# A list-scheduled hybrid encoder layer on one core: the steps that finish and store the output are given earlier due times, and in the last block of the down projection the B12 sums are made by accumulating DMAs

## The chip, the core and the metric

One core of one Trainium2 chip runs the whole layer. Its engines are TensorE (PE, with its weight loads, PEld), VectorE (DVE), ScalarE (ACT), GpSimd (POOL) and SyncE (SP); SP issues most DMAs, and POOL issues those that add into their destination. Each engine runs its instructions in the order in which they stand in the program, and waits for the others by semaphores. The metric is the device time of one execution in microseconds (us); the median of three runs counts.

## The reference, cut to what matters

```
mod = silu(c) @ w_ada + b_ada;  sh1, sc1, gt1, sh2, sc2, gt2 = split(mod, 6)
h = rmsnorm(x, g_norm_mix) * (1 + sc1) + sh1
proj = h @ w_in            # 2048 -> 1024 (RG-LRU) + 1024 (its gate) + 1024 (pooling)
y = concat(rg_lru(conv(xr)) * gelu(gr), pool_mixer(xp)) @ w_out
x = x + gt1 * y
h = rmsnorm(x, g_norm_ffn) * (1 + sc2) + sh2
f = (silu(h @ w_ffn_gate) * (h @ w_ffn_up)) @ w_ffn_down      # 2048 -> 5632 -> 2048
x = x + gt2 * f
return rmsnorm(x, g_norm_final)                                # (1, 512, 2048), float32
```

One sequence of 512 tokens, model width 2048, everything in float32. The change concerns the last line but one and the last: the product with w_ffn_down, the gate gt2, the residual sum and the final norm.

## The kernel before

**Products.** A float32 product is made of three passes on TensorE: each operand is split into `hi` (a rounded copy, made by ACT) and `lo` (the rest, made by DVE), and hi·hi, hi·lo and lo·hi are summed in PSUM (`mm3x`). The three FFN products go by `seven` (line 879): a block matrix product of 2 by 2 blocks in seven products instead of eight, called A11, n1, s2, n4, A12, n3 and A22 after their left operand. Each right operand is built in SBUF from four weight blocks B11, B12, B21 and B22 of 128 x 1024 elements (512 KB): `b11(i)` loads B11 into a buffer `araw` (`chain`) and splits its negative; `t1(i)` adds B12 to it and splits the sum; `t2(i)` adds B22, which lies in a buffer `raw` (`other`); `b22(i)` splits that; `t3(i)` adds B12 to it and splits; `b21(i)` loads B21 into `raw` and subtracts it in the chain; `t4(i)` splits what the chain has become. So B12 is added twice in each part i. `plus_b12` (line 916) has two ways for it: with `by_dma` a DMA issued by POOL adds the block from HBM into the buffer, without it SP loads the block into a `raw` buffer and DVE adds. The gate and up projections use the first way, the down projection the second. There are four `araw` buffers, six `raw`, and three each of `hi` and `lo`.

**The down projection** runs in four blocks of the 5632 inner channels (DOWN_BLOCKS 2, 3, 3, 3). The last block has three parts i, and it goes over the output in two halves `qp` of 1024 columns; a half is 7 products of 3 parts with 12 matmuls each, 252 matmuls of 128 x 512. The output lies in 16 tiles `fsum[t][q]` of 128 x 512 (t: 4 token tiles, q: 4 quarters of the columns; `qa`, `qb` are a half's two). In the names that follow the four tiles of q=1 are b_2454, b_2455, b_2446, b_2447, those of q=0 b_2436, b_2437, b_2478, b_2479, those of q=3 b_2506, b_2507, b_2498, b_2499, and those of q=2 b_2488, b_2489, b_2530, b_2531. `later_block` adds the products' PSUM banks to them, and in the last block, when a tile is complete, it calls `finish`: `residual` multiplies the tile by the gate (DVE) and adds x1 from HBM by an accumulating DMA of 256 KB (POOL); ACT sums the squares; DVE multiplies by the final norm's weight `gfin[q]`; and when the last quarter of a token tile is done, `norm` computes the factor 1/rms, scales the four tiles (one on DVE, three on ACT) and stores them (SP). For the last quarter, q=2, residual comes early and `finish` multiplies the product's PSUM bank by the gate and adds it. The gates (`gt_0` to `gt_3`) and `gfin` come by eight DMAs of 256 KB into buffers `blk`.

**The order.** The code does not run as written: `Program` records all instructions with an estimated cost, `deadlines` gives each a due time, counted back from what needs it, and `schedule` plays the engines forward in a model and always takes the instruction that can start first, among equals the one with the earlier due time. The result is one fixed order for each engine. A rule in `buffers` (line 269) bears on the DMAs into `blk`: `dma_free` is the time up to which the model has the DMA engines filled, `now` is the time of the queue that would issue, and while the first is over DMA_AHEAD = 4 us ahead of the second and the load isn't overdue, the load is not taken:

```
if op["dma"] and tag == "blk" and dma_free - now > self.DMA_AHEAD and late > 0.0 and not wide:
    return need, None
```

`wide` becomes true only when nothing else can go on any engine. The model charges a DMA from POOL at twice the time of one from SP.

Of the kernel before, what the change touches and what calls it, by code (L numbers as in the profile page):

```python
# [27 lines left out]
ADA_CHUNKS = (1, 1, 2, 2, 2, 2, 2, 2, 2)  # L28
GROUP_ENDS = (2, 8, 16)
HELD = 6  # L30
NFF = 5632 // 512
DOWN_BLOCKS = (2, 3, 3, 3)
BUFS = {"blk": 69, "raw": 6, "araw": 4, "hi": 3, "lo": 3, "acc": 6, "mm": 2}
# [3 lines left out]
class Program:  # L37
# [35 lines left out]

    def __init__(self, nc, bufs, spare):
        self.nc, self.bufs, self.spare = nc, bufs, spare
        self.ops, self.tags, self.in_order = [], {}, set()
        for q in self.QUEUES:
            setattr(self, q, self.Queue(self, q))

# [15 lines left out]
    def add(self, queue, method, args, kw):  # L95
        after, lead = kw.pop("after", None), kw.pop("lead", None)
        outs = list(args[:1]) + [kw[n] for n in ("out", "accum_out") if kw.get(n) is not None]
        ins = list(args[1:]) + [v for n, v in kw.items() if n not in ("out", "accum_out")] + [after]
        on_chip = lambda v: isinstance(v, bass.AP) and type(v.tensor).__name__ == "Tile"
        op = {"i": len(self.ops), "q": self.QUEUES[queue], "call": (queue, method, args, kw),  # L100
              "w": [self.region(v) for v in outs if on_chip(v)], "r": [self.region(v) for v in ins if on_chip(v)]}
        if op["q"] == "PE":
            op["w"] = [(name, 0, P, 0, 512) for name, *_ in op["w"]]
        op["tiles"] = list(dict.fromkeys(x[0] for x in op["w"] + op["r"] if x[0] in self.tags))
        op["t"], op["stream"] = self.cost(op["q"], method, args, kw, outs[0])
        reads = [v for v in ins if on_chip(v) and v.space not in (bass.MemoryType.PSUM, bass.MemoryType.DRAM) and v.shape[-1] > 1]
        op["dma"] = method == "dma_start"
        op["port"] = op["q"] == "POOL" and len(reads) > 0 and not op["dma"] or op["q"] == "DVE" and (
            len(reads) > 1 or len(reads) == 1 and method in ("tensor_scalar", "tensor_copy"))
        op["table"], op["lead"] = self.TABLES.get(kw.get("func")), lead  # L110
        self.ops.append(op)

    @staticmethod
# [41 lines left out]
    def deadlines(self):  # L155

        at = 0.0
        users, order, serves = {}, {}, {}
        for op in self.ops:
            op["due"] = 1e9  # L160
            if op["q"] == "PE":
                op["due"] = op["nominal"] = at
                at += op["t"]
            for name in op["tiles"]:
                tag = self.tags[name]
                if name not in users and tag != "blk":
                    tiles = order.setdefault(tag, [])
                    if len(tiles) >= self.bufs[tag]:
                        for i in users[tiles[-self.bufs[tag]]]:
                            serves.setdefault(i, []).append(op["i"])  # L170
                    tiles.append(name)
                users.setdefault(name, []).append(op["i"])
        before = [set(op["pred"]) for op in self.ops]
        for i, later in serves.items():
            for j in later:
                if j > i:
                    before[j].add(i)
        behind = [0] * len(self.ops)
        for js in before:
            for j in js:  # L180
                behind[j] += 1
        latest, queued, held = [at + 50.0] * len(self.ops), {}, {}
        heap = [(-latest[i], -i) for i, n in enumerate(behind) if not n]
        heapq.heapify(heap)
        while heap:
            _, i = heapq.heappop(heap)
            op = self.ops[i := -i]
            q, due = op["q"], latest[i]
            tag = self.tags.get(op["w"][0][0]) if q == "SP" and op["w"] else None
            if tag in ("raw", "araw"):  # L190
                due = queued[tag] = min(due, queued.get(tag, 1e9) - 0.6)
            op["due"] = min(op["due"], due - op["t"] - (self.SLACK if not op["dma"] else self.SLACK_DMA if q == "SP" else self.SLACK_SUM))
            if q in ("DVE", "ACT", "SP"):
                t = max(op["t"], self.DMA_ISSUE) if q == "SP" else op["t"] * self.LOAD
                op["due"] = held[q] = min(op["due"], held.get(q, 1e9) - t)
            for j in before[i]:
                latest[j] = min(latest[j], op["due"])
                behind[j] -= 1
                if not behind[j]:
                    heapq.heappush(heap, (-latest[j], -j))  # L200
        for op in self.ops:
            if op["lead"] is not None:
                op["due"] = op["lead"] - 1e3 + 1e-4 * op["i"]

# [158 lines left out]
def hybrid_trunk(ctx: ExitStack, tc: tile.TileContext, a: dict, out: bass.AP):  # L363
# [6 lines left out]
    nc = Program(tc.nc, BUFS, SPARE)  # L370
# [189 lines left out]
    proj = {}  # L560
    held = {n: mmps("acc") for n in range(HELD)}

# [145 lines left out]
    def pool_group(g):  # L708
# [16 lines left out]
        for j in range(2):  # L725
            ps = mmps()
            for k in range(2):
# [11 lines left out]
                  lead=3)  # L739
# [237 lines left out]
    left = []  # L977
# [71 lines left out]
    kept = None  # L1049
    for n in range(NFF):  # L1050
        f = gate_up(n, kept)
        kept = lambda n=n, f=f: keep(n, f)
# [5 lines left out]
    for bi, nb in enumerate(DOWN_BLOCKS):  # L1058
        last = bi == len(DOWN_BLOCKS) - 1
        left = []  # L1060
# [13 lines left out]
        for qp in range(2):  # L1074
# [67 lines left out]
            def later_block(step, banks, tiles=range(2)):  # L1142
                for j in tiles:
                    x, y = banks["X"][j], banks.get("Y", (None, None))[j]
                    if step == "P1":
                        add(j, qa, x, ALU.subtract)
                        if last and qp:
                            residual(j, qa)
                    elif step == "G5":
                        add(j + 2, qb, y)  # L1150
                    elif step == "G6":
                        add(j, qb, x)
                    elif step == "G3":
                        add(j, qb, y)
                    elif step == "G7":
                        add(j + 2, qb, x)
                    elif last and qp:
                        finish(*((j, qa, banks["Z"][j]) if step == "P2" else (j + 2, qa, x)))
                    elif step == "P2":
                        add(j, qa, banks["Z"][j])  # L1160
                    else:
                        add(j + 2, qa, x, ALU.subtract)
                    if last and (step in ("G3", "G7") or step in ("P2", "G4") and not qp):
                        finish(*{"G3": (j, qb), "G7": (j + 2, qb), "P2": (j, qa), "G4": (j + 2, qa)}[step])
# [5 lines left out]
            if last and qp:  # L1170
                for t in (2, 3):
                    residual(t, qa)
            seven(left, b, later_block if bi else first_block, False, by_tile=last and qp == 1, within=kept if not bi and not qp else None)
        n0 += nb

    nc.issue()
# [22 lines left out]
```

## Time and profile before

| | us |
|---|---|
| median of 3 runs | 1877.52 (1876.21 to 1879.55) |
| the profiled execution, its own time | 1870.78 |
| its span, first to last instruction | 1868.9 |
| PE busy | 1797.6 (96%) |
| DVE busy | 1540.0 (82%) |
| ACT busy | 935.9 (50%) |
| POOL busy | 196.3 (11%) |

The times below are counted from the start of the span of the profiled execution. A row of the timeline reads: start, duration, engine, line (every recorded instruction has the helper's line 359 before and 361 after), operation, output<-input, shape, count, and in brackets how long the engine had been idle and what ended that. A row of the waits reads: who waited for whom, total, times, longest. "DMA to landing" is the time from the issue of a DMA to its completion. PEclk is the granted clock of TensorE as a share of 2.4 GHz.

### The profile page before, as it was taken

The numbers are of one execution on the slowest core, as the hardware profiler recorded it, in microseconds if no ns is written. First come the engines' busy times: TensorE is split into PE (matmuls) and PEld (weight loads), VectorE is DVE, ScalarE is ACT, GpSimd is POOL, SyncE is SP. The second block draws the span as 40 slices with busy tenths as digits, with TensorE's granted clock in tenths as the row PEclk, the third lists the DMA queues.
The fourth block names the chain that finished last, engine by engine and source line by source line (L and its number), as shares of the span: only waits on it lengthen the run. The fifth ranks groups of instructions, "written<-read, shape, count | busy, mean of one in ns | idle before, by whom it ended". The sixth has DMA issues, their size and how long they took to land.

```text
span 1868.9 us, 22751 instructions
## 1 busy us (share of the span) xinstructions
PE 1797.6 (96%) x8011; PEld 1469.1 (79%) x8011; DVE 1540.0 (82%) x1974; ACT 935.9 (50%) x1221; POOL 196.3 (11%) x192
## 2 busy tenths in 40 slices
PE   3899998899999999999999999999999999999996
PEld 2687877688886888888788888888888888888875
DVE  5899998899969878678787867877678887878897
ACT  7435794422377555454454545545455543333345
POOL 0000054500001111111111111111110000000011
PEclk9999999999999999999999999999999999999998
DMA  9999755499945777788878778777799966947556
GB/s 304 315 359 321 227 175 184 142 334 342 359 146 104 192 201 213 209 207 214 221 191 226 208 205 214 210 202 199 171 273 318 339 218 195 328 155 263 194 143 180
DMA packets 285763, 429.97 MB, mean 230 GB/s; under 512 B 20760, under 2 KB 119760, under 8 KB 285648
## 3 DMA queue, kind: packets, MB, share of 16 engines
q1 hardware_dynamic: 259408, 378.17, 60.4%
q0 software_dynamic: 26240, 50.34, 16.2%
q8 instruction: 63, 1.03, 0.2%
q14 instruction: 52, 0.43, 0.1%
HBM read 378.63 MB, written 49.81 MB: 229 GB/s over the span
## 4 chain that ended last, share of the span: by engine, by line
PE 65%; DVE 15%; issue 9%; DMA 7%; ACT 2%; SPq 1%; POOL 1%; ACTq 0%; DVEq 0%; POOLq 0%
PE acc L359 62%; DVE b L359 10%; DVE lo L359 4%; DMA araw<-in_w_ada 3%; PE mm L359 3%; ACT b L359 2%; SPq L359 1%; DVE araw L359 1%; DMA b<-x 1%; DMA raw<-in_w_ffn_down 1%; ACT hi L359 1%; DMA b<-in_x 1%; DMA araw<-in_w_ffn_up 1%; DMA raw<-in_w_ffn_gate 0%; DMA araw<-in_w_ffn_gate 0%
## 5 line engine op out<-in xcount | busy, mean ns | idle before, releaser
L359 PE MATMUL acc<-hi,b 128*128 128x512 f32 x4208 | 1290.0, 392 | 1.6 <-DVE b L359 1.0
L359 PEld LDWEIGHTS acc<-hi,b 128*128 128x128 f32 x4208 | 789.7, 188 | 166.2 <-DVE b L359 2.5
L359 PE MATMUL acc<-lo,b 128*128 128x512 f32 x2104 | 803.1, 393 | 4.7 <-DVE lo L359 4.5
L359 ACT ACTIVATE hi<-raw 128x1024 fp32r<-128x1024 f32 (+2 forms) x297 | 306.5, 1034 | 436.6 <-PE acc L359 347.2
L359 PEld LDWEIGHTS acc<-lo,b 128*128 128x128 f32 x2104 | 395.3, 188 | 91.2 <-DVE lo L359 10.6
L359 DVE TENSOR_TENSOR lo<-raw,hi 128x1024 fp32r<-128x1024 f32 (+2 forms) x297 | 355.4, 1199 | 126.1 <-ACT hi L359 125.1
L359 ACT ACTIVATE hi<-araw 128x1024 fp32r<-128x1024 f32 x264 | 279.8, 1060 | 286.4 <-PE acc L359 268.9
L359 DVE TENSOR_TENSOR lo<-araw,hi 128x1024 fp32r<-128x1024 f32 x198 | 241.9, 1222 | 57.0 <-ACT hi L359 56.5
L359 DVE SCALAR_TENSOR_TENSOR b<-araw,c_act,b 128x512 f32<-128x512 f32 (+1 forms) x315 | 233.0, 746 | 8.0 <-DMA araw<-in_w_ada 4.7
L359 DVE TENSOR_TENSOR b<-b,b 128x512 f32<-128x512 f32 (+4 forms) x318 | 195.0, 634 | 14.2 <-ACT b L359 10.7
L359 PE MATMUL acc<-b,hi 128*128 128x512 f32 x608 | 189.2, 396 | 4.0 <-ACT hi L359 1.5
L359 ACT ACTIVATE b<-b 128x512 fp32r<-128x512 f32 (+2 forms) x223 | 128.6, 596 | 97.7 <-DVE b L359 54.9
L359 PEld LDWEIGHTS acc<-b,hi 128*128 128x128 f32 x608 | 114.3, 190 | 31.0 <-ACT b L359 3.5
L359 DVE SCALAR_TENSOR_TENSOR lo<-araw,hi 128x1024 fp32r<-128x1024 f32 x66 | 80.6, 1223 | 47.6 <-ACT hi L359 47.4
L359 PE MATMUL acc<-b,lo 128*128 128x512 f32 x304 | 116.1, 396 | 2.5 <-DVE lo L359 2.5
L359 POOL DMA_DIRECT2D araw<-in_w_ffn_up x44 | 53.1, 1209 | 557.8 <-DVE lo L359 390.4
L359 ACT ACTIVATE b<-acc 128x512 f32<-128x512 f32 x142 | 81.7, 593 | 53.9 <-PE acc L359 45.5
L359 DVE TENSOR_TENSOR araw<-araw,raw 128x1024 f32<-128x1024 f32 x88 | 106.9, 1220 | 0.6
L359 DVE SCALAR_TENSOR_TENSOR araw<-araw,raw 128x1024 f32<-128x1024 f32 x66 | 79.9, 1220 | 13.6 <-DMA raw<-in_w_ffn_gate 8.6
L359 POOL DMA_DIRECT2D raw<-in_w_ffn_up x44 | 53.0, 1204 | 334.4 <-DVE lo L359 332.9
L359 PE MATMUL mm<-b,hi 128*128 128x512 f32 x192 | 62.2, 404 | 10.4 <-ACT b L359 10.3
L359 PEld LDWEIGHTS acc<-b,lo 128*128 128x128 f32 x304 | 58.1, 191 | 15.8 <-DVE lo L359 3.8
(72 smaller groups left out, 872.8 us busy)
## 6 DMA issues: line engine op xcount, KB each, us to landing
araw<-in_w_ada SPq DMA_DIRECT2D x256, 256.0 KB, 4.6
raw<-in_w_ffn_down SPq DMA_DIRECT2D x88, 512.0 KB, 5.5
f<-b SPq DMA_DIRECT2D x154, 256.0 KB, 4.7
b<-f SPq DMA_DIRECT2D x154, 256.0 KB, 5.9
araw<-in_w_ffn_gate SPq DMA_DIRECT2D x44, 512.0 KB, 3.8
raw<-in_w_ffn_up SPq DMA_DIRECT2D x44, 512.0 KB, 4.2
araw<-in_w_ffn_up POOLq DMA_DIRECT2D x44, 512.0 KB, 7.0
raw<-in_w_ffn_gate SPq DMA_DIRECT2D x44, 512.0 KB, 5.7
```

Of the source, the lines that this page charges most:

```text
L359: getattr(getattr(self.nc, queue), method)(*args, **kw)
```

## The change

Three edits. (1) A constant END_EARLY = 60.0; while `nc.early` is set, recorded instructions carry it, and at the end of `deadlines` their due time is made 60 us earlier. It is set round the `finish` calls of the last half's steps P2 and G4, those that complete the four tiles of q=2 and call `norm`, so their products with the gate, squares, factors, scalings and output DMAs carry it. (2) The last block of the down projection is called with `by_dma` true: the 12 B12 blocks of its two halves are no longer loaded by SP and added by DVE, but added by 12 accumulating DMAs of 512 KB from POOL. (3) Nothing else is computed or left out.

```diff
+END_EARLY = 60.0
...
-        self.ops, self.tags, self.in_order = [], {}, set()
+        self.ops, self.tags, self.in_order, self.early = [], {}, set(), 0.0
...
-        op["table"], op["lead"] = self.TABLES.get(kw.get("func")), lead
+        op["table"], op["lead"], op["early"] = self.TABLES.get(kw.get("func")), lead, self.early
...
         for op in self.ops:
+            op["due"] -= op["early"]
             if op["lead"] is not None:
...
                     elif last and qp:
+                        nc.early = END_EARLY
                         finish(*((j, qa, banks["Z"][j]) if step == "P2" else (j + 2, qa, x)))
+                        nc.early = 0.0
...
-            seven(left, b, later_block if bi else first_block, False, by_tile=last and qp == 1, within=kept if not bi and not qp else None)
+            seven(left, b, later_block if bi else first_block, last, by_tile=last and qp == 1, within=kept if not bi and not qp else None)
```

What this does to the orders shows at three places. First DVE, in the last block's first half, as its last B21 blocks and the A22 operands are split; the tiles b_24xx are those of q=1 and q=0, b_2954 is gate gt_1 and b_2911 the norm weight of q=1. Before:

```order
L359 TENSOR_TENSOR b_2455<-b_2455,acc_2929 128x512
L359 TENSOR_TENSOR b_2454<-b_2454,b_2954 128x512
L359 TENSOR_TENSOR lo_2972<-raw_2970,hi_2971 128x1024
L359 TENSOR_TENSOR b_2455<-b_2455,b_2954 128x512
L359 TENSOR_TENSOR lo_2975<-raw_2973,hi_2974 128x1024
L359 TENSOR_TENSOR b_2446<-b_2446,acc_2917 128x512
L359 TENSOR_TENSOR b_2447<-b_2447,acc_2918 128x512
L359 TENSOR_TENSOR b_2446<-b_2446,b_2954 128x512
L359 TENSOR_TENSOR lo_2978<-raw_2976,hi_2977 128x1024
L359 TENSOR_TENSOR b_2447<-b_2447,b_2954 128x512
L359 TENSOR_TENSOR b_2454<-b_2454,b_2911 128x512
```

The products with gate and norm weight stand between the splits here. Now the same tiles (the gate gt_1 is called b_2951) stand at the end of DVE's order, behind the very last split of the program, lo_3055 (the third part of the second half's A22 operand):

```order
L361 TENSOR_TENSOR lo_3053<-araw_2990,hi_3052 128x1024
L361 TENSOR_TENSOR b_2499<-b_2499,acc_2986 128x512
L361 TENSOR_TENSOR lo_3055<-araw_2993,hi_3054 128x1024
L361 TENSOR_TENSOR b_2454<-b_2454,b_2951 128x512
L361 TENSOR_TENSOR b_2455<-b_2455,b_2951 128x512
L361 TENSOR_TENSOR b_2446<-b_2446,b_2951 128x512
L361 TENSOR_TENSOR b_2447<-b_2447,b_2951 128x512
L361 TENSOR_TENSOR b_2454<-b_2454,b_2911 128x512
L361 TENSOR_TENSOR b_2455<-b_2455,b_2911 128x512
L361 TENSOR_TENSOR b_2446<-b_2446,b_2911 128x512
L361 TENSOR_TENSOR b_2447<-b_2447,b_2911 128x512
L361 TENSOR_TENSOR b_2436<-b_2436,b_2973 128x512
```

All 12 tiles of q=1, 0 and 3 moved there in this pattern, four products with the gate and then four with the norm weight, and the four tiles of q=2 stand behind them. Second, SP's queue, where the gates and norm weights (gt, in_g_norm_final) are loaded. Before, the first of them stood among the loads of the last block's first half:

```order
L359 DMA b_2909<-f_1173 128x512
L359 DMA b_2954<-gt_1_1175 128x512
L359 DMA araw_2993<-in_w_ffn_down 128x2x512
L359 DMA raw_2957<-in_w_ffn_down 128x2x512
L359 DMA b_2913<-in_g_norm_final 128x512
L359 DMA b_2910<-in_g_norm_final 128x512
L359 DMA b_2911<-in_g_norm_final 128x512
L359 DMA b_2912<-in_g_norm_final 128x512
```

Now all eight follow the last weight block of the program (raw_3030, a B21 block of the second half):

```order
L361 DMA raw_3024<-in_w_ffn_down 128x2x512
L361 DMA raw_3027<-in_w_ffn_down 128x2x512
L361 DMA raw_3030<-in_w_ffn_down 128x2x512
L361 DMA b_2951<-gt_1_1175 128x512
L361 DMA b_2910<-in_g_norm_final 128x512
L361 DMA b_2911<-in_g_norm_final 128x512
L361 DMA b_2912<-in_g_norm_final 128x512
L361 DMA b_2913<-in_g_norm_final 128x512
L361 DMA b_2973<-gt_0_1174 128x512
L361 DMA b_3019<-gt_3_1177 128x512
L361 DMA b_2984<-gt_2_1176 128x512
L361 DMA out<-b_2498 128x512
```

The loads of gates and norm weights have moved behind all weight loads, next to the stores of the output. Third, POOL's queue behind the up projection. Before, the sixteen residual sums (x_t_q) followed at once; now the twelve B12 sums stand ahead of them, of which these are the last six:

```order
L361 DMA araw_2987<-in_w_ffn_down 128x2x512
L361 DMA araw_2990<-in_w_ffn_down 128x2x512
L361 DMA araw_2993<-in_w_ffn_down 128x2x512
L361 DMA raw_3004<-in_w_ffn_down 128x2x512
L361 DMA raw_3007<-in_w_ffn_down 128x2x512
L361 DMA raw_3010<-in_w_ffn_down 128x2x512
L361 DMA b_2454<-x_0_1_705 128x512
L361 DMA b_2455<-x_1_1_709 128x512
```

The first residual sum now comes behind the last B12 sum, which belongs to step G7 of the second half.

## Rows read from the trace of the kernel before

**Rows 1.** The profile's page: span; busy time and share of each engine

```profile
span 1868.9 us, 22751 instructions
...
PE 1797.6 (96%) x8011; PEld 1469.1 (79%) x8011; DVE 1540.0 (82%) x1974; ACT 935.9 (50%) x1221; POOL 196.3 (11%) x192
```

**Rows 2.** Stretches near the end: busy time by engine, PEclk, DMA share, GB/s

```profile
1820.00:1830.00 10.00, 10.00 (x45) 7.98 (x44) 9.86 (x12) 3.56 (x4) 1.35 (x2) 1.00 0.41 131
...
1840.00:1850.00 10.00, 9.03 (x32) 6.99 (x32) 10.00 (x16) 6.42 (x12) 2.39 (x3) 0.83 0.37 52
...
1860.00:1865.00 5.00, 0.00 (x0) 0.00 (x0) 2.05 (x8) 3.64 (x7) 0.00 (x0) 0.50 0.91 305
```

**Rows 3.** Timeline of PE in the last block

```profile
1755.04 0.62 PE L359 MATMUL acc<-hi,b 128*128 128x512 f32 x2
...
1755.72 0.62 PE L359 MATMUL acc<-hi,b 128*128 128x512 f32 x2
...
1797.30 0.50 PE L359 MATMUL acc<-lo,b 128*128 128x512 f32 x1 [0.84 <-DVE lo L359]
...
1840.63 0.73 PE L359 MATMUL acc<-lo,b 128*128 128x512 f32 x2 [2.01 <-DVE lo L359]
...
1842.17 1.48 PE L359 MATMUL acc<-hi,b 128*128 128x512 f32 x3
...
1856.66 0.39 PE L359 MATMUL acc<-hi,b 128*128 128x512 f32 x1
```

**Rows 4.** Timeline of ACT in the last block

```profile
1736.43 1.07 ACT L359 ACTIVATE hi<-araw 128x1024 fp32r<-128x1024 f32 x1 [1.21 <-PE acc L359]
...
1781.29 0.63 ACT L359 ACTIVATE b<-b 128x512 f32<-128x512 f32 x1 [3.00 <-DMA b<-x]
1781.82 0.19 ACT L359 ACTIVATION_READ_ACCUMULATOR b<-b 128x1 f32 x1
...
1860.99 2.72 ACT L359 ACTIVATE b<-b,s 128x512 f32<-128x512 f32 x4
```

**Rows 5.** Timeline of DVE in the last block

```profile
1732.08 1.23 DVE L359 SCALAR_TENSOR_TENSOR lo<-araw,hi 128x1024 fp32r<-128x1024 f32 x1 [1.49 <-ACT hi L359]
...
1777.94 0.68 DVE L359 TENSOR_TENSOR b<-b,b 128x512 f32<-128x512 f32 x1
...
1782.04 0.69 DVE L359 TENSOR_TENSOR b<-b,b 128x512 f32<-128x512 f32 x1 [1.68 <-ACT b L359]
...
1842.82 3.09 DVE L359 TENSOR_TENSOR b<-b,b 128x512 f32<-128x512 f32 x5
...
1851.38 1.21 DVE L359 TENSOR_TENSOR lo<-araw,hi 128x1024 fp32r<-128x1024 f32 x1
...
1858.32 0.69 DVE L359 TENSOR_TENSOR b<-b,b 128x512 f32<-128x512 f32 x1
```

**Rows 6.** Timeline of POOL: issues of residual sums

```profile
1778.92 0.86 POOL L359 DMA_DIRECT2D b<-x  x1 [2.07 <-DVE b L359]
...
1828.65 1.77 POOL L359 DMA_DIRECT2D b<-x  x2 [15.90 <-DVE b L359]
```

**Rows 7.** POOL DMAs to landing: residual sums, B12 into araw, into raw

```profile
DMA to landing us min/median/max: 4.0/4.9/7.7
...
DMA to landing us min/median/max: 5.8/7.0/11.4
...
DMA to landing us min/median/max: 5.9/6.2/11.8
```

**Rows 8.** The page: DMA queue, packets, MB, share of 16 engines

```profile
q0 software_dynamic: 26240, 50.34, 16.2%
```

**Rows 9.** Groups of DVE by line and form, 1737 to 1869 us

```profile
L359 DVE TENSOR_TENSOR araw<-araw,raw 128x1024 f32<-128x1024 f32 x11 | 13.2, 1220 | 0.0
...
L359 DVE TENSOR_TENSOR raw<-raw,raw 128x1024 f32<-128x1024 f32 x6 | 7.3, 1221 | 1.7 <-DMA raw<-in_w_ffn_down 1.7
```

**Rows 10.** Waits, 1700 to 1869 us

```profile
ACT b L359 <- DMA b<-x: 21.6, 9, 4.3
```

## The prediction, made before the changed kernel ran

> **What bounds the kernel now.** I read the page first: PE is busy for 96% of the span, DVE for 82%, POOL for 11% [rows 1]. So up to the end TensorE sets the time, and an edit that takes work from DVE can give back only what PE waits for DVE. I then went to the last block, the only place where the change moves much. The stretches show three phases [rows 2]: PE without a gap beside a DVE at 9.86 of 10 us, then 1840 to 1850 with PE at 9.03 and a granted clock of 0.83, then, from 1860 on, no PE at all, and the time goes to factors, scalings and stores. PE's timeline gives the size of the gaps: 0.84 us at 1797 and 2.01 us at 1841, both ended by a `lo` of DVE, and behind the second three matmuls take 1.48 us, where three normally follow each other in 0.68 (1755.04 to 1755.72) [rows 3]; the clock had been full until that gap and fell in the stretch that holds it, to a mean of 0.83, so part of it ran at 1.2 instead of 2.4 GHz. PE ends at 1856.66 + 0.39 = 1857.05. From there to the end of the span are 11.85 us.
>
> How much is there to win? ACT's split at 1736.43 waits for a buffer that PE gives up with its last matmul of the block before [rows 4], so the last block starts there. It has 2 halves x 7 products x 3 parts x 12 matmuls = 504, at 0.68/3 = 0.227 us [rows 3] 114.3 us: unhindered PE would end at 1850.7. The gaps of the whole last block are thus 6.4 us, and no more than that lies in a faster DVE.
>
> **The change: what it removes.** Twelve additions of 1.22 us leave DVE, 14.6 us [rows 9]; beside them PE is busy, so what they are worth is in the 6.4 us and is not counted twice. The second gap hangs on a raw block that comes late and is added on DVE; in the new order the block's B12 goes into its buffer by POOL, a product earlier. I take both gaps as gone.
>
> **What it adds on POOL.** Twelve accumulating DMAs of 512 KB. The 88 of this kind in the trace land 7.0 (into `araw`) or 6.2 us (into `raw`) after issue, 11.4 and 11.8 at most [rows 7]. Behind `t1` or `t3` waits the split, behind that PE. A product of three parts lasts 36 x 0.227 = 8.2 us, and the split of B11 ends at 1732.08 + 1.23 = 1733.3, 3.1 us before PE starts on it at 1736.4 [rows 4, 5]; so there are 11.3 us from the split to the next product. Needed are 0.3 us to the issue, 7.0 to landing, and 1.07 + 1.23 for the next two splits [rows 4, 5]: 9.6. At the median it fits by 1.7 us, at the largest landing it is short by about 3. It is short in up to three of the four places (the `t3` of the second half has another product between). That is 0 to 9 us; most of the 88 lie near the median, so I take 2 us. PE's end comes to 1850.7 + 2 = 1852.7.
>
> **What it moves, and this decides.** In the order shown, the products of the 12 tiles of q=1, 0 and 3 with gate and norm weight, and everything for q=2, stand behind the last split, lo_3055. Before, they stood between the splits. DVE runs in order, so nothing of it starts earlier, even though the gates will have landed long before. Before, the last split ended at 1851.38 + 1.21 = 1852.6, 4.5 us ahead of PE's end [rows 3, 5]. With three buffers for `hi` and `lo` it can't run further ahead now: the last part's buffer is freed only when PE leaves n3. So the tail starts at about 1852.7 - 4.5 = 1848.2. Its working, from there:
>
> A group of four tiles is: four products with the gate, four residual sums by POOL, four squares on ACT, four products with the norm weight; and the next group's gate products stand behind these. The first gate product ends after 0.7 us; POOL starts 0.3 us behind it (1777.94 + 0.68 = 1778.62 to 1778.92) [rows 5, 6]. A residual sum lands 4.0 us after issue at the least, 4.9 in the median, 7.7 at most [rows 7]; with no other traffic I take 4.1. Four in a burst don't all take 4.1: POOL can issue one every 0.88 us (two in 1.77) [rows 6], but its queue moved 50.34 MB in 16.2% of 1868.9 us, which is 6.0 us per MB [rows 8], 1.6 us for 256 KB. So the fourth lands at 1.0 + 4.1 + 3 x 1.6 = 9.9. Square and its read-out end 0.75 us later, since the read-out starts at 1781.82 after a square begun at 1781.29 and DVE goes on at 1782.04 [rows 4, 5]; the last product with the norm weight takes the 0.6 us that lie between starts (3.09 for five) [rows 5]. A group takes 11.3 us, three groups 33.9.
>
> The last group, q=2: four products of PSUM banks and the first gate product, 3.1 us; POOL 0.3; first landing 4.1; three more at 1.6; the last addition 0.7: 13.0 us. Before, the end of that addition (1858.32 + 0.69) lay 9.9 us ahead of the end of the span [rows 1, 5]. Now ACT has all twelve scalings behind it, where before six had been done; six at 2.72/4 = 0.68 [rows 4] add 4.1. So 27.0 us.
>
> The sum: 1848.2 + 33.9 + 27.0 = 1909.1, against a span of 1868.9: +40.2 us. The profiled execution took 1870.78, the median of the runs is 6.74 us above; I add the difference to the median: 1877.5 + 40.2 = **1918 us**, 2.1% slower. The two ends: with no wait of PE, landings of 4.0 us and a burst at POOL's pace (9.0 a group, 24.8 for the last) the span is 1846.2 + 27.0 + 24.8 = 1898, time 1907. With 7 us of waits, the median landing of 4.9 and 2 us between landings (13.3 a group, 29 for the last) it is 1853.2 + 39.9 + 29 = 1922, time 1931.
>
> The early due times gain nothing here: an instruction can only be preferred once its inputs are there, and the q=2 steps need the gate gt_2, whose load is the last of SP's in the order shown. ACT's 21.6 us of waiting for residual sums [rows 10] cost nothing before, because splits went on between them; at the end of the order the same waits have no cover.
>
> The trace has residual sums of 256 KB at 4.0 to 7.7 us, and B12 sums of 512 KB at medians of 7.0 and 6.2 [rows 7]. The Trainium skill, "DMA: Bandwidth & Descriptors", section "Anatomy of one DMA — SWDGE (gpsimd) path", gives a fit for a DMA from POOL of about 2.0 us plus its bytes at 436 GB/s, an estimate of 2.6 and 3.2 us here. The trace disagrees with it in all 104 sums. By the fit the groups would take 7.6 us, the last 23.3, and the time would be 1903; case (b) below is as near to that as the rows allow.
>
> **The rivals.** (a) The B12 sums are late at every product: 9 us instead of 2, place `t1` and `t3`. For it speaks the short slack of 1.7 us and the maximum of 11.8, and that SP's loads run beside it; against it that products of four parts in the up projection have not shown it. Time 1918 + 7 = 1925. (b) The landings of a burst overlap, 4.0 us after each issue: groups of 9.0, a last group of 24.8, from 1848.2: span 1900, time 1909. It would need a queue that moves twice what it moved on average. (c) The other side: the tail does not lie behind PE. This needs DVE to have the last split done by 1868.9 - 60.9 = 1808, more than 40 us before PE's end; then PE and the old tail would decide, 1850.7 + 11.85 = 1862.5, time 1871. Against it stand the three `hi` and `lo` buffers. A tail in which no wait at all remained would still have 40 instructions x 0.6 us on DVE, 2 us of small ones, and 5.2 us from the last scaling (1860.99 + 2.72) to the end [rows 4, 5]: 1846.2 + 31.2 = 1877, still 8 us over the span of before. (d) The change doesn't do what it says: the sums are not faster by DMA and the rest stays; excluded by the order, except for a gap in my reading of it.
>
> **How the numbers follow.** The forecast 0.75, (a) 0.10, (b) 0.12, (c) 0.02, (d) 0.01. Forecast, (a) and (b) lie between 1907 and 1931, which is the range. A measurement can tell about 0.2% (4 us) from no change; faster 0.02, within it 0.01, slower 0.97.
>
> **What would show it.** After: PE's end earlier, near 1851 to 1855, and no PE for some 55 us behind it; in this stretch DVE in four short bursts with waits for squares and residual sums between them, POOL four issues at a time; no 2 us gap of PE in the second half; a clock at 1.0 until PE ends. If PE's end is later than 1857, the B12 sums are late. If the groups take under 9 us, my landings are too long; if PE runs on to the end of the span, the reading of the order is wrong, and with it the sum.

## The result and the profile after

The changed kernel takes 1925.95 us (1923.47 to 1928.72) beside 1876.87 us (1873.36 to 1879.55) of the kernel before: ratio 1.0265, interval 1.0243 to 1.0287, 49 us slower. 1918 was predicted, with 1907 to 1931 as the range. The profiled execution took 1925.73 us, with a span of 1923.9.

On the page of the changed kernel, PE's busy time is what it was [rows 1], DVE has 12 us less, and the span is 55 us longer. In the row of forty slices PE stands at 9 from the ninth to the 38th, then at 7 and at 0: the time was added behind PE.

```profile
span 1923.9 us, 22754 instructions
...
PE 1796.7 (93%) x8011; PEld 1470.5 (76%) x8011; DVE 1528.1 (79%) x1962; ACT 937.4 (49%) x1221; POOL 211.6 (11%) x204
...
PE   3899998899999999999999999999999999999970
```

To compare runs, one needs a mark that the executions have in common. ACT's split that [rows 4] shows at 1736.43 waits for PE's last matmul of the block before; here it starts at 1743.92 (first row below). The 7.5 us between the two arise before the last block, in a part that the change hardly touches; an unchanged kernel, run once more below, came to the same split at 1741.07, and in the fourteen traces of this document it lies anywhere from 1735.4 to 1746.7. So I count from this split on. (It is the third of the block's splits of B11. The expectations call it the last block's first split; what makes it a mark is that it waits for the last matmul of the block before.) The timeline of ACT, then of PE, in the last block of the changed kernel:

```profile
1743.92 1.06 ACT L361 ACTIVATE hi<-araw 128x1024 fp32r<-128x1024 f32 x1 [1.66 <-PE acc L361]
...
1809.73 1.06 ACT L361 ACTIVATE hi<-araw 128x1024 fp32r<-128x1024 f32 x1 [6.39 <-PE acc L361]
1813.64 1.06 ACT L361 ACTIVATE hi<-araw 128x1024 fp32r<-128x1024 f32 x1 [2.85 <-DMA araw<-in_w_ffn_down]
1817.57 2.95 ACT L361 ACTIVATE hi<-araw 128x1024 fp32r<-128x1024 f32 x3 [2.88 <-DMA araw<-in_w_ffn_down]
```

```profile
1795.35 0.97 PE L361 MATMUL acc<-hi,b 128*128 128x512 f32 x3 [0.84 <-DMA b<-f]
...
1863.21 0.39 PE L361 MATMUL acc<-hi,b 128*128 128x512 f32 x1
```

PE ends at 1863.21 + 0.39 = 1863.60, 119.7 us after the mark; before it was 1857.05 - 1736.43 = 120.6 [rows 3, 4]. From PE's end to the end of the span are 60.3 us, where there were 11.9. From the mark to the end: 180.0 against 132.5 us, 47.5 more, and all of it in the tail.

DVE's timeline of that tail. The row at 1857.23 is the last split, lo_3055:

```profile
1857.23 1.23 DVE L361 TENSOR_TENSOR lo<-araw,hi 128x1024 fp32r<-128x1024 f32 x1 [0.22 <-ACT hi L361]
1858.37 2.49 DVE L361 TENSOR_TENSOR b<-b,b 128x512 f32<-128x512 f32 x4
1864.43 0.69 DVE L361 TENSOR_TENSOR b<-b,b 128x512 f32<-128x512 f32 x1 [3.57 <-ACT b L361]
...
1869.71 3.10 DVE L361 TENSOR_TENSOR b<-b,b 128x512 f32<-128x512 f32 x5 [0.64 <-ACT b L361]
...
1882.08 3.10 DVE L361 TENSOR_TENSOR b<-b,b 128x512 f32<-128x512 f32 x5 [0.65 <-ACT b L361]
...
1894.66 1.28 DVE L361 TENSOR_TENSOR b<-acc,b 128x512 f32<-128x512 f32 x2
...
1907.28 0.69 DVE L361 TENSOR_TENSOR b<-b,b 128x512 f32<-128x512 f32 x1
```

POOL's timeline (issues of accumulating DMAs): three of the twelve new sums, then the residual sums in four bursts:

```profile
1799.87 1.21 POOL L361 DMA_DIRECT2D araw<-in_w_ffn_down  x1 [27.31 <-DVE lo L361]
1802.18 1.20 POOL L361 DMA_DIRECT2D araw<-in_w_ffn_down  x1 [1.09 <-DVE lo L361]
1804.90 1.20 POOL L361 DMA_DIRECT2D araw<-in_w_ffn_down  x1 [1.52 <-DVE lo L361]
...
1859.61 3.55 POOL L361 DMA_DIRECT2D b<-x  x4 [24.46 <-DVE b L361]
1871.30 3.59 POOL L361 DMA_DIRECT2D b<-x  x4 [8.14 <-DVE b L361]
1883.88 3.52 POOL L361 DMA_DIRECT2D b<-x  x4 [9.00 <-DVE b L361]
1898.03 3.52 POOL L361 DMA_DIRECT2D b<-x  x4 [10.62 <-DVE b L361]
```

Four products, four issues, squares and products with the norm weight, and then the next four: three groups and a last one, as read from the order. The gate products start at 1858.37, 12.0 us later in the second group (the last four of the five from 1869.71), 12.4 later in the third, and the PSUM products at 1894.66. From the end of the last split (1858.46) to 1894.66 are 36.2 us, from there to the end 29.2.

The stretches (columns as in [rows 2]) show what PE lost before that:

```profile
1790.00:1800.00 10.00, 9.16 (x40) 7.24 (x40) 4.87 (x5) 3.52 (x4) 0.13 (x1) 1.00 0.91 292
1800.00:1810.00 10.00, 10.00 (x45) 8.26 (x45) 3.65 (x4) 1.95 (x3) 3.49 (x3) 1.00 1.06 305
1810.00:1820.00 10.00, 7.54 (x28) 4.43 (x26) 7.34 (x8) 4.27 (x5) 0.00 (x0) 1.00 0.86 218
```

From 1810 to 1820 PE issued 28 matmuls where it issues 45 in others. DVE was busy for 7.34 us there, so the cause isn't DVE's load any more. The three B12 sums issued at 1799.87, 1802.18 and 1804.90 are split at 1809.73, 1813.64 and 1817.57: 9.9, 11.5 and 12.7 us later. (The bracket of the first of these splits names PE, but its sum landed only 0.1 us before it started; the three landed 9.8, 11.4 and 12.6 us after their issue.) The DMA engines were busy all the while (0.91, 1.06, 0.86), and SP's timeline says with what:

```profile
1738.57 1.40 SPq L361 DMA_DIRECT2D b<-f  x2
1789.86 0.38 SPq L361 DMA_DIRECT2D araw<-in_w_ffn_down  x1
...
1790.85 1.46 SPq L361 DMA_DIRECT2D raw<-in_w_ffn_down  x3
...
1793.14 2.12 SPq L361 DMA_DIRECT2D raw<-in_w_ffn_down  x3
...
1796.65 5.60 SPq L361 DMA_DIRECT2D b<-in_g_norm_final  x4
1803.08 4.54 SPq L361 DMA_DIRECT2D b<-gt  x3
```

For 50 us SP issues nothing; then all that is left of the kernel's loads goes out within 18 us, the eight loads of gates and norm rows (1795.37 to 1807.62) among it. SP's waits give the reason, one wait of 49.8 us for a split that has to read a buffer first:

```profile
SPq L361 <- DVE lo L361: 52.1, 2, 49.8
```

### The profile page after: what moved, and what is told of

The parts are those of the page before. It is cut to its first block, busy times and chain, and to the rows that moved or that the text cites. A ratio compares the mean times of both kernels' runs of the same rounds, so it can differ in the third digit from the quotient of the medians.

```text
span 1923.9 us, 22754 instructions
## 1 busy us (share of the span) xinstructions
PE 1796.7 (93%) x8011; PEld 1470.5 (76%) x8011; DVE 1528.1 (79%) x1962; ACT 937.4 (49%) x1221; POOL 211.6 (11%) x204
## 5 line engine op out<-in xcount | busy, mean ns | idle before, releaser
L361 PEld LDWEIGHTS acc<-hi,b 128*128 128x128 f32 x4208 | 789.9, 188 | 168.2 <-ACT hi L361 2.6
L361 DVE SCALAR_TENSOR_TENSOR b<-araw,c_act,b 128x512 f32<-128x512 f32 (+1 forms) x315 | 232.8, 745 | 14.1 <-DMA araw<-in_w_ada 11.0
L361 DVE TENSOR_TENSOR araw<-araw,raw 128x1024 f32<-128x1024 f32 x82 | 99.7, 1219 | 0.6
```

The costliest lines, as they stand in the source:

```text
L361: getattr(getattr(self.nc, queue), method)(*args, **kw)
```

## The experiments

Theory: the loss is the place of the last steps, behind the last split, and it comes from the second edit: with the sums on POOL the scheduler's rule at L271 and L272 of the changed code (a `blk` load isn't taken while modelled transfers reach 4 us beyond the queue's clock) holds the eight loads of gates and norm rows back until nothing else can go, and then, by the code, takes one at a time, and each gate releases four tiles. Rivals: the early due times; the accumulating DMAs themselves. The diffs are against the changed kernel.

**Each edit alone.** only_early takes the second edit back:

```
-            seven(left, b, later_block if bi else first_block, last, by_tile=last and qp == 1, within=kept if not bi and not qp else None)
+            seven(left, b, later_block if bi else first_block, False, by_tile=last and qp == 1, within=kept if not bi and not qp else None)
```

> The change without its second edit: END_EARLY stays 60, the B12 sums go back to VectorE. Theory (the whole loss comes from the second edit, by where it puts the last steps; early due times gain nothing): the last steps stay between the splits, PE's end and the 11.9 us behind it stay as before, so 1873 to 1879 against 1876.9. Rival (the early due times pull the last steps about): over 1890, with more than 20 us between PE's end and the end of the span.

Measured: 1878.46 us beside 1874.02, ratio 1.0023 (1.0008 to 1.0038). The rival is out: 14.1 us lie behind PE's end, not over 20. only_dma takes the first edit back (`END_EARLY = 0.0`):

> The change without its first edit: END_EARLY 0, the B12 sums of the last block by accumulating DMAs. Theory: 1926, within 4 us of the changed kernel, with the same four bursts behind PE. If early due times matter here: more than 5 us away from 1926.

Measured: 1921.21 us, 1.0253 (1.0231 to 1.0275), 177.9 us from the mark to the end and the same four bursts (the last as three and one). The time is 4.7 us under the 1926 that were expected within 4, but the ratio, beside other runs of the kernel before, agrees with the changed kernel's 1.0265 within the intervals. The second edit alone does it.

**The same sums, the last steps back in their place.** gates_free exempts the eight loads from the rule (they are tagged with an advance of 100 that isn't subtracted):

```
-            op["due"] -= op["early"]
+            op["due"] -= op["early"] % 100.0
...
-                if op["dma"] and tag == "blk" and dma_free - now > self.DMA_AHEAD and late > 0.0 and not wide:
+                if op["dma"] and tag == "blk" and op["early"] < 100.0 and dma_free - now > self.DMA_AHEAD and late > 0.0 and not wide:
...
-            gfin = []
+            gfin, nc.early = [], 100.0
...
+            nc.early = 0.0
...
                     gt2[q] = blk()
+                    nc.early += 100.0
                     nc.sync.dma_start(out=gt2[q], in_=gt2_kept[q])
+                    nc.early -= 100.0
```

> Both edits as in the changed kernel, but the eight loads of the gates and of the last norm's rows are exempt from the scheduler's rule that holds a load of this pool back while transfers are queued. With that the last steps stand between the splits again, though the sums stay accumulating DMAs. Theory (the 49 us are the tail behind PE, the sums themselves cost next to nothing: from the last block's first split to PE's end the changed kernel took 119.7 us, the kernel before 120.7): 1872 to 1880, with some 12 us behind PE's end. Rival (the accumulating DMAs are what costs, by sums that come late): over 1895, with PE waiting for splits in the last block. Between: each microsecond over 1880 is one that the sums cost.

Measured: 1879.21 us, 1.0030 (1.0016 to 1.0044), with 12.9 us behind PE's end. So of the 49 us, 44 go with the place of the last steps. PE's end is at 123.9 us from the mark, not earlier than before.

**The last steps late, without any new sum.** only_late is the kernel before, with the eight loads, tagged as in gates_free, not taken before all matmuls are placed (`END_EARLY` is 0 here):

```
-                if op["dma"] and tag == "blk" and dma_free - now > self.DMA_AHEAD and late > 0.0 and not wide:
+                if op["dma"] and tag == "blk" and not wide and (pace if op["early"] >= 100.0 else dma_free - now > self.DMA_AHEAD and late > 0.0):
...
-            seven(left, b, later_block if bi else first_block, last, by_tile=last and qp == 1, within=kept if not bi and not qp else None)
+            seven(left, b, later_block if bi else first_block, False, by_tile=last and qp == 1, within=kept if not bi and not qp else None)
```

> The kernel before, without either edit, but with the same eight loads held until the scheduler has placed all matmuls: the last steps go behind the last split, as in the changed kernel, in one burst of sixteen residuals, and no accumulating DMA is added. Theory (the place of the last steps costs): 16 issues x 0.88 = 14.1 us on POOL, 7 us for the first product and the last landing, and the 16.6 us that the changed kernel shows from the last landing to the end: 38 us from the last split, which ends 4.5 us ahead of PE; 33 behind PE where the kernel before has 11.9: 1877 + 21 = 1898, 1890 to 1910. If the three groups of four are needed for the whole loss, this run shows what is left without them: the changed kernel's 1926 less 24 = 1902. Rival (the sums are the cause): 1877.

Measured: 1895.80 us, 1.0109 (1.0084 to 1.0134), some 21 us slower. That is the expected number, but by luck: two errors cancel in it. Its timelines of ACT, PE and POOL show them, in this order:

```profile
1746.70 1.07 ACT L361 ACTIVATE hi<-araw 128x1024 fp32r<-128x1024 f32 x1 [1.21 <-PE acc L361]
```

```profile
1860.57 0.39 PE L361 MATMUL acc<-hi,b 128*128 128x512 f32 x1
```

```profile
1856.96 10.68 POOL L361 DMA_DIRECT2D b<-x  x12 [454.31 <-DVE b L361]
```

PE's end lies 1860.96 - 1746.70 = 114.3 us behind the mark: the 504 matmuls at 0.227 us of the prediction, with no wait left. So it was the last steps between the splits that cost the kernel before its 6.3 us at PE. The expectation had left PE's end where it was. And 39.8 us follow behind PE's end, where 33 were expected: 27.9 more than before, less the 6.3 that PE gains. The residuals go in one stream here, and yet the place alone costs 21 us net. The expectation had reckoned with POOL's issues, 0.88 us each; the stretches (columns as in [rows 2]) and the landings of the sixteen show another limit:

```profile
1860.00:1870.00 10.00, 0.95 (x5) 0.45 (x3) 8.96 (x16) 2.17 (x6) 9.11 (x11) 0.79 1.10 189
1870.00:1880.00 10.00, 0.00 (x0) 0.00 (x0) 4.87 (x9) 2.90 (x9) 1.97 (x3) 0.50 1.12 201
...
DMA to landing us min/median/max: 4.2/9.7/10.9
```

The DMA engines are full, at 189 to 201 GB/s, which is 1.3 to 1.4 us for each sum of 256 KB: the sixteen land 1.4 us apart in the mean, from 1861.13 to 1881.78, though POOL issues the first twelve within 10.68 us.

**Which sums are late?** gates_free0 is gates_free with `END_EARLY = 0.0`; gf0_t3 has only T3's six sums by DMA besides; late_t1 and late_t3 are only_late with T1's six or T3's six (`last and "t1"` or `"t3"` in the call of `seven`):

```
-            if by_dma:
+            if by_dma is True or by_dma == ("t1" if part is chain[i] else "t3"):
```

> The changed kernel with the eight loads exempt from the scheduler's rule, as before, and END_EARLY 0: the sums by accumulating DMAs alone, with the last steps between the splits. Theory (the sums come late and cost PE 5.4 to 6.3 us: from the last block's first split to PE's end 114.3 us without sums and without last steps, 120.6 and 119.7 with the sums; and the 14.6 us that they take off VectorE give back about as much, since the kernel before loses 6.3 us there to its last steps): 1872 to 1879, ratio 0.999 to 1.003. Rival (the early due times, which put last steps ahead of the last splits, were the 4 to 5 us that both runs with END_EARLY 60 lost): ratio under 1.001, with 3 us less than the run with END_EARLY 60.

> As the run before, but only the second sums of each half (the six of T3, into the tile of B22) go by accumulating DMAs; the six of T1 are on VectorE. Theory (a T1 sum can only start when the split of B11 has read its tile, one product of 11.3 us ahead, in both halves; a T3 sum has one product in the first half and two in the second, where A12 stands between): T1's sums are the late ones, so this loses less than 3 us at PE for 7.3 us off VectorE: ratio 0.997 to 1.000, the version of these that could beat the kernel before. Rival (any accumulating DMA here is as bad as another): ratio 1.000 to 1.003 as with all twelve.

> The run with the last steps held back, in which PE never waits in the last block (114.3 us from the first split to PE's end), with the six T1 sums of that block by accumulating DMAs. Theory (T1's sums are the late ones): 118 to 120 us from the first split to PE's end, with ScalarE's split of the sum waiting for a DMA. Rival (all twelve cost alike, about 0.5 us each): 117.

> The same with the six T3 sums instead. Theory: 114.5 to 117 us, with a wait only in the first half. Rival: 117, with waits in both halves.

Measured: gates_free0 1.0034 (1.0018 to 1.0049), a little over the expected range, so the early due times were not what gates_free lost; gf0_t3 1.0022 (1.0007 to 1.0037), PE's end 120.5 us from the mark, no gain. late_t1 and late_t3 (one execution each, 1895.6 and 1907.1 us) both have PE's end at 114.3 us. My theory that T1's sums are late fell, and with it the rival that each sum costs half a microsecond: six cost nothing, whichever six. That left both together:

> The run with the last steps held back, with all twelve sums of the last block by accumulating DMAs: it closes the square of none (114.3 us from the first split to PE's end), the six of T1 (114.3) and the six of T3 (114.3). The recorded order has the residuals in three bursts of four, four and eight, as with T3 alone. Theory (only both together cost: without the twelve temporary tiles the loads of the second half go out in one bunch, and T1's sums land in it): 119 to 121 us from the first split to PE's end, T1's sums of the second half split 10 us or more after their issue, where with T1 alone they took 6.0; from the last split to the end 52 us as with T3 alone, 171 us in all from the first split, ratio to the kernel before 1.020. Rival (the twelve sums are free, and the 5.4 to 6.3 us of the changed order came from the gate loads, which stand in the same bunch there too, or from the order of its last steps): 114.3.

late_both is only_late with the call of the changed kernel (`last`). Measured: 1909.52 us, 1.0175 (1.0135 to 1.0215); PE's end at 1863.75, 120.5 us from the mark at 1743.22. So none, T1 and T3 give 114.3, both 120.5. Beside it, T1's sums of the second half in late_t1, where they cost nothing; POOL's issues, then ACT's splits of these sums, then two stretches:

```profile
1794.20 1.19 POOL L361 DMA_DIRECT2D araw<-in_w_ffn_down  x1 [50.49 <-DVE lo L361]
1796.92 1.19 POOL L361 DMA_DIRECT2D araw<-in_w_ffn_down  x1 [1.53 <-DVE lo L361]
1799.64 1.21 POOL L361 DMA_DIRECT2D araw<-in_w_ffn_down  x1 [1.53 <-DVE lo L361]
```

```profile
1800.05 1.06 ACT L361 ACTIVATE hi<-araw 128x1024 fp32r<-128x1024 f32 x1 [1.97 <-DMA araw<-in_w_ffn_down]
1803.10 1.06 ACT L361 ACTIVATE hi<-araw 128x1024 fp32r<-128x1024 f32 x1 [1.99 <-DMA araw<-in_w_ffn_down]
1805.62 1.06 ACT L361 ACTIVATE hi<-araw 128x1024 fp32r<-128x1024 f32 x1 [1.46 <-DMA araw<-in_w_ffn_down]
```

```profile
1790.00:1800.00 10.00, 10.00 (x46) 8.27 (x45) 6.04 (x6) 3.18 (x3) 2.74 (x3) 1.00 0.53 111
1800.00:1810.00 10.00, 10.00 (x46) 8.29 (x45) 8.26 (x9) 4.25 (x4) 0.85 (x1) 1.00 0.55 97
```

5.9, 6.2 and 6.0 us from issue to split, beside DMA engines that are busy for half of the time, against 9.9 to 12.7 in the changed kernel, 10.6 to 13.2 in late_both, beside full ones. SP's timelines, of late_t1 and then of late_both, show why the engines differ:

```profile
1762.54 20.87 SPq L361 DMA_DIRECT2D raw<-in_w_ffn_down  x9
```

```profile
1794.61 0.76 SPq L361 DMA_DIRECT2D b<-gt  x1
1796.08 6.17 SPq L361 DMA_DIRECT2D b<-in_g_norm_final  x4
1803.09 4.99 SPq L361 DMA_DIRECT2D b<-gt  x3
```

With T1 alone, SP still loads six temporary tiles for T3's sums on DVE, as buffers come free, and its loads spread over the half. With T3 alone SP runs into one wait of 40.4 us, with both into one of 49.9 us, and then issues all that is left at once. As these timelines read, T3's sums by DMA make the bunch, and T1's sums land in it where they are DMAs too: that would be why only both together cost.

This is read from the DMA shares and the queues beside the landings; no run took the bunch away and left the twelve sums. Nor does late_both rule out the rival with the gate loads: as the rows show, all eight stand in its bunch as well, while late_t1 issues them from 1829.70 on. gates_free0 answers a part of it. There five of the eight are loaded some 50 us earlier, and T1's sums of the second half still take 9.6, 10.6 and 10.5 us to the split, beside DMA engines at 0.93 to 1.12. Which of the other loads matter stays open.

The bursts of late_both and late_t3 are four, four and eight. POOL in late_t3:

```profile
1854.17 3.52 POOL L361 DMA_DIRECT2D b<-x  x4 [24.24 <-DVE b L361]
1864.06 3.47 POOL L361 DMA_DIRECT2D b<-x  x4 [6.38 <-DVE b L361]
1875.08 6.97 POOL L361 DMA_DIRECT2D b<-x  x8 [7.55 <-DVE b L361]
```

That gives the price of a round trip. From the end of the last split to the end of the span: 45.0 us (only_late) and 44.8 (late_t1) with one stream of residuals, 52.3 (late_t3) and 52.8 (late_both) with three bursts, 62.4 (only_dma) and 65.4 (the changed kernel) with four.

**A version that could be faster, and a control.** t1_dma is the kernel before with T1's six sums by DMA and the rule as it was. control is the kernel before with an unused name at its end; early_again is only_early once more.

> The kernel before with only the six T1 sums of the last block by accumulating DMAs, no early due times and the scheduler's rule as it was; the recorded order keeps the last steps between the splits. Theory (six T1 sums alone cost PE nothing, as with the last steps held back, where it ended 114.3 us after the first split, and they take 7.3 us off a VectorE whose last steps cost the kernel before 6.3 us there): PE's end 115 to 119 us after the first split, ratio to the control 0.997 to 1.000. Rival (the residuals and the sums share one queue, so that either is late): PE's end at 121 or more, ratio over 1.001.

> The kernel before once more, with one unused name at its end: no instruction differs. It shows what the comparison gives for no change. Expected ratio 0.999 to 1.001. If it is over 1.0015, the 0.2 to 0.3 per cent of the runs with small changes are the comparison's own and not theirs.

> END_EARLY 60 alone, once more, beside the control. Only some 40 instructions of VectorE in the last 20 us stand in another order, and in the first profile of it the stretch from the last block's first split to the end took 132.6 us, as in the kernel before (132.5). Theory (it costs nothing): the same ratio as the control's, within 0.0015. Rival (it costs 4 us, as its first comparison says): 1.002 more than the control.

Measured: t1_dma 1875.75 us, 1.0011 (0.9996 to 1.0026), PE's end 119.5 us from the mark, where 115 to 119 were expected; control 1876.84 us, 1.0014 (1.0000 to 1.0029); early_again 1874.34 us, 1.0011 (0.9996 to 1.0027). No change measures 0.14% here. So neither only_early nor gf0_t3 can be told from the kernel before, gates_free and gates_free0 hardly, and t1_dma isn't shown to be faster. Its T1 sums are not free: in the second half they stand between residual sums in POOL's queue, take 6.1, 8.4 and 9.3 us from issue to split, and PE waits for 1.32 and 0.76 us there. Control in its timelines of ACT and PE:

```profile
1741.07 1.06 ACT L359 ACTIVATE hi<-araw 128x1024 fp32r<-128x1024 f32 x1 [1.21 <-PE acc L359]
```

```profile
1861.11 0.39 PE L359 MATMUL acc<-hi,b 128*128 128x512 f32 x1
```

The traces, counted from the mark, repeat better than the times: 120.4 and 11.9 us here (span 1873.4), 120.6 and 11.9 in the profile before, although the mark itself lies 4.6 us apart. The two traces of only_early (early_again is the second), though, differ by 1.1 us in all, and the remaining kernels were traced once each, so about 1 us is what this measure can tell apart; t1_dma's gain in it is no larger. In that measure, for all kernels (us; each from the same three rows as above, mark, last matmul and span; in only_dma and late_both the split at the mark starts 0.3 and 0.2 us later than PE's pace would have it):

| kernel | sums by DMA | last steps | mark to PE's end | PE's end to end | in all |
|---|---|---|---|---|---|
| before | none | between splits | 120.6 | 11.9 | 132.5 |
| control | none | between splits | 120.4 | 11.9 | 132.3 |
| only_early | none | between, early | 118.5 | 14.1 | 132.6 |
| early_again | none | between, early | 119.1 | 14.6 | 133.7 |
| t1_dma | T1 | between | 119.5 | 11.8 | 131.3 |
| gf0_t3 | T3 | between | 120.5 | 13.2 | 133.7 |
| gates_free0 | both | between | 122.1 | 12.4 | 134.5 |
| gates_free | both | between, early | 123.9 | 12.9 | 136.8 |
| only_late | none | behind, one stream | 114.3 | 39.8 | 154.1 |
| late_t1 | T1 | behind, one stream | 114.3 | 39.7 | 153.9 |
| late_t3 | T3 | behind, 3 bursts | 114.3 | 47.2 | 161.5 |
| late_both | both | behind, 3 bursts | 120.5 | 47.7 | 168.2 |
| only_dma | both | behind, 4 bursts | 120.6 | 57.3 | 177.9 |
| changed | both | behind, 4 bursts | 119.7 | 60.3 | 180.0 |

## Why the prediction was right, and where its terms were off

**Direction and mechanism: right.** The tail lies behind the last split and has no cover: 60.3 us behind PE's end (56.4 predicted, 1909.1 - 1852.7), DVE in four bursts, POOL four issues at a time. gates_free and only_late are the proof from both sides: the same sums with the last steps in place cost some 5 us at most, late steps without a sum 21. That the change costs 49 and not 21 us is mostly the groups of four, which the prediction also had; the order has them because the scheduler's model takes one gate load at a time. On the chip all eight loads were issued by 1807.62 (SP's rows above), 50 us before the first product with a gate.

**The sum, term by term.** From the mark, 172.7 us were predicted (1909.1 - 1736.43) and 180.0 measured. The 7.3 us are these:
- PE's end: 116.3 predicted (114.3 + 2), 119.7 measured, +3.4.
- Last split to PE's end: 4.5 predicted, 5.1 measured, -0.6.
- Three groups: 33.9 predicted, 36.2 measured, +2.3. The first landing was right: 4.1 us from the issue at 1859.61 to the square at 1863.68. The groups are about 12 us instead of 11.3, mostly because the four landings of a group are not 1.6 us apart but 1.7 to 2.0 in the mean: 2.1 to 3.5 us to the second, then 1.3 to 1.7 each.
- Last group to the end: 27.0 predicted, 29.2 measured, +2.2. The last addition ends at 1907.97, 15.9 us ahead of the end, where 14.0 were taken. I had added only what is scaled later; ACT's twelve scalings take 7.5 us from 1909.81 on, and SP's sixteen stores, all of them in one row, 9.0 us from 1910.55 on.

**"I take both gaps as gone": wrong.** The old gaps did go, as only_late shows best (114.3), since the last steps no longer stand between the splits, and not because the B12 additions left DVE, as the prediction has it: only_late keeps all twelve of them there. New ones came: 0.84 us behind the load of a left part at 1795.35, and some 17 matmuls from 1810 to 1820. The step that failed is the slack. I set 11.3 us of slack against 9.6 needed, with landings of 7.0 us from 88 sums of the up projection [rows 7], and didn't ask what removing twelve loads does to SP's queue: SP's other loads go out in a bunch, and T1's sums of the second half, beside it, take 9.8 to 12.6 us to land. Of the four places only this one was short; in the other three the sums landed in 5.8 to 8.1 us and PE did not wait. The prediction even named the sign, "if PE's end is later than 1857, the B12 sums are late"; 1863.6 is later, but 7.5 us of that were there at the mark, so the sign should have been set from the mark (over 116.3). As for the price, 5.4 us lie between the 2 taken and the upper end of 7.

**Rival (a)**, the sums late at every product, would have given 1925, and 1926 was measured; but it is not what happened. PE lost 5.4 us and not 9; with the last steps behind the splits T3's sums by themselves cost nothing, nor did T1's by themselves. The other half of the miss is in the tail. **Rival (b)**, landings that overlap fully in groups of 9.0 us, is out for the groups. The 1.6 us between landings that I took from the queue's average was near: 1.4 in the mean in one stream with full DMA engines (only_late), 1.7 to 2.0 in the groups. POOL's issues, one every 0.89 us, say nothing of it. At 1.4 us each sixteen landings take some 21 us in any order (an estimate); the rounds add to that, since the DMA engines are idle for a part of each, as this stretch of the changed kernel shows with 0.70 beside the 1.12 of only_late:

```profile
1870.00:1880.00 10.00, 0.00 (x0) 0.00 (x0) 4.04 (x7) 1.46 (x5) 3.49 (x4) 0.50 0.70 105
```

**(c)** and **(d)** did not happen.

**Early due times gain nothing:** right for the time, for another reason than given. In the changed kernel the stretch from the mark to the end is 2.1 us longer with them than without (180.0 and 177.9, one trace each). Alone they do move the last steps: PE's end comes 1.3 to 2.1 us earlier from the mark, and 2.2 to 2.7 us more follow behind it.

**The median:** I added 6.74 us to the profiled execution, because it lay that far under the median. Control's profiled execution took 4.4 us more than the one before, and its mark lies 4.6 us later: scatter from before the last block.

The Trainium skill's fit for a DMA from POOL ("DMA: Bandwidth & Descriptors", section "Anatomy of one DMA — SWDGE (gpsimd) path"), which the prediction set against the rows, gives an estimate of 3.2 us for 512 KB. The traces disagree again: 5.9 us to the split was the shortest of T1's sums in the rows above, 13.2 the longest.

## What to carry to other kernels

Work that is taken off a busy engine also changes what the queues and the scheduler see: look for what the removed loads had spaced out, and for rules that compare with a queue's backlog. Steps with a round trip (product, accumulating DMA, square) belong between other work; behind everything else they cost 21 us net here even in one stream, whose sixteen landings by themselves kept the DMA engines full for some 21 us; three and four bursts cost 7 to 20 us more. For such a stream count landings and not issues. Count from a mark inside the program when the stretch before it scatters more than the effect.

## What the runs showed of the hardware

An accumulating DMA of 512 KB took 6 us beside half-busy DMA engines (late_t1) and 10 to 13 us beside full ones (the changed kernel and late_both). While only such sums ran (1830 to 1840 of the changed kernel), the engines were busy at 0.93 and moved 157 GB/s by the profile's count; plain loads in late_t1 moved 401 at 1.05:

```profile
1830.00:1840.00 10.00, 10.00 (x46) 8.28 (x45) 7.29 (x9) 4.05 (x4) 2.95 (x3) 1.00 0.93 157
```

```profile
1725.00:1735.00 10.00, 10.00 (x46) 8.29 (x45) 5.92 (x6) 3.73 (x4) 0.00 (x0) 1.00 1.05 401
```

So by these two stretches a sum by DMA takes more than twice the engines' time of the load that it replaces. That had not entered my sum. The residual sums of 256 KB bear it out: with full engines they moved 189 to 201 GB/s in only_late.
